# Four sums of the last pair on VectorE, and a matmul of the forget gates one token tile later

## The chip, the cores and the metric

The kernel runs on one core of a Trainium2 chip. The metric is the device time of one execution in microseconds (us), as a median over runs. The engines are named as in the profile: PE is TensorE (PEld its weight loads), DVE is VectorE, ACT is ScalarE, POOL is GpSimd, and SP is SyncE, which only issues transfers here. L1408 means line 1408 of the kernel before.

## The reference

A decoder trunk of two layers on 1024 tokens of width 1024. Layer 0 mixes tokens by sparse attention, layer 1 by attention with forget gates; both end with a gated ConvFFN. Two places of it matter here: the ConvFFN's last product, and the forget gates of layer 1.

```python
def conv_ffn(h, w_up, conv_w, conv_b, w_down):      # D_FF = 2816
    u = h @ w_up                                     # 1024 x 5632
    u = lax.conv_general_dilated(u, conv_w[:, None, :], ...) + conv_b   # causal, depthwise, width 3
    a, b = u[..., :D_FF], u[..., D_FF:]
    return (jax.nn.silu(a) * b) @ w_down             # 1024 x 2816 @ 2816 x 1024

# reference(), before layer 1
hs = rms_norm(x, kv_norm) @ w_kv_shared              # keys, values, 12 gate columns
log_f = jax.nn.log_sigmoid(hs[..., 2 * MIX_W:].astype(jnp.float32) + b_fgate.astype(jnp.float32))
dcum = jnp.cumsum(log_f, axis=1).transpose(0, 2, 1)  # added to the attention's scores
```

## The kernel before

**Precision.** Every f32 operand of a large matmul is split into a high and a low half (`split`: ACT writes the high half at L81, DVE the low half at L82), and a product is three matmuls (`mm3`, L157 to L159).

**The ConvFFN.** Both of its products are computed with seven block products in place of eight, so sums of blocks are needed on each side. `Up` makes the hidden values in 22 chunks of 128 columns, as tiles of 128 columns by 1024 tokens (names `v`). Two neighbouring chunks `g` and `h` make a pair; there are 11 pairs, numbered 0 to 10. `left(k)` makes the left factors of pair k: four of the seven are sums (`s1`, `s2`, `s4` and an upper half of `g`, written in place), made by the four adds of L1408 to L1411 on tiles of 128x512, and three are the halves of `g` and `h` themselves. `store(k)` writes all seven to DRAM (`gd`, L1417), in the order of `self.factors`: two halves of `v` first, then `s2` and the rest. For pairs 0 to 9 the sums lie in tiles `gs`, for pair 10 in tiles `ws`.

**The down product.** `Down` works in steps: one step is one block product i of one pair j, 12 matmuls of 128x512 (four row blocks, three matmuls each). The steps are, in order, product 0 with pairs 0 to 9 (steps 0 to 9 here), product 1 with pairs 0 to 9 (steps 10 to 19), product 0 and product 1 with pair 10 (steps 20 and 21), and then the other five products (step 22 on). A step needs a left factor, read back from `gd` into a tile `wr` (`fetch`, L1508; one tile holds the factors of two steps; there are three such tiles), and a block of `w_down` (in tiles `hx` and `hT`, loaded at L1497). `prep` splits both into a `wh` and a `wl`, of which there are four each: the split of step n + 4 can start when PE has left step n. Sums of `w_down` blocks for later steps are adds on DVE (L1529, L1531, L1533).

**What sets the order.** Within `Up.run` the instructions of DVE and ACT keep the order in which the code records them, by slots (`manual_schedule` in `gated`): pair 10 has `left` in slot 164 and `store` in slot 166, the down steps start in slot 160. On POOL, PE and SP a scheduler sets the order when the kernel is built, as it does for all that is recorded after `Up.run`; of that it fills some in ahead, such as the sums L1529. Each engine works through its own list in that order. SP's is the one queue for all transfers: a transfer that waits for its data holds up all that stand behind it. The factors of pair 10 and the fetches of the following steps stand like this on SP in layer 0 (`gd_10` is the DRAM tile of pair 10, and `wr_11351` takes the factors of steps 14 and 15); the change leaves these rows as they are:

```order
L1508 DMA wr_11304<-gd_2_9070 128x512
L1508 DMA wr_11304<-gd_3_9353 128x512
L1417 DMA gd_10_11337<-v_11048 128x512
L1417 DMA gd_10_11337<-v_11178 128x512
L1417 DMA gd_10_11337<-ws_11292 128x512
L1417 DMA gd_10_11337<-v_11048 128x512
L1417 DMA gd_10_11337<-v_11178 128x512
L1417 DMA gd_10_11337<-ws_11292 128x512
L1417 DMA gd_10_11337<-ws_11293 128x512
L1508 DMA wr_11351<-gd_4_9636 128x512
L1508 DMA wr_11351<-gd_5_9919 128x512
L1508 DMA wr_11406<-gd_6_10202 128x512
```

The fetches for steps 14 to 19 stand behind the store of pair 10.

**The forget gates.** `middle` ends with two rounds over the eight token tiles: the first round (n = 0) computes the first part of the values and the gate columns `z`, the second (n = 1) the rest of the values; a tile is 24 matmuls of 128x390 (`layer1_v`). Around the second round stands the generator `forget`, in three parts. Part one turns `z` into log sigmoids `lsg`, on ACT and with some 17 small instructions on DVE (L992 to L1003). Part two makes their running sum with four matmuls against a triangle and ones (L1008, L1009) and a few small adds (L1013, L1014). Part three transposes the result (L1020) and stores it to `dd` (L1026), which the attention reads later (L1079, L1087). L1198 says ahead of which tile each part comes: 0, 2 and 4.

## Time and profile before

| | |
|---|---|
| median of 3 runs | 2561.35 us (2555.23 to 2565.48) |
| profiled execution, its own time | 2560.4 us |
| its span in the trace | 2558.4 us |
| mean granted clock of PE | 0.993 |
| busy: PE, PEld | 2460.7 us, 2052.7 us |
| busy: DVE, ACT, POOL | 1868.4 us, 1345.1 us, 764.1 us |

The span runs from the first to the last instruction in the trace; the 2.0 us beside it are the start and end of an execution. A row of the timeline reads: start in us, duration in us, engine, line, operation, tile written and tiles read, shape, count, and in brackets how long the engine was idle before and what ended that. A row of the chain of waits has start, duration, and what the chain ran through; "issue" is time in which the engine waited for nothing that the profile shows. Matmuls overlap, so the duration of one (0.39 us) is longer than the distance from its start to the next start.

### The profile page before, as it was taken

The page shows a single profiled execution, that of the slowest core. Times are in us where ns is not written, and L with a number is a line of the kernel's source. Part 1 is how long each engine was busy: PE and PEld are TensorE (multiplying, and loading weights), DVE is VectorE, ACT ScalarE, POOL GpSimd, SP SyncE. Part 2 cuts the span into 40 slices and gives each one's busy share as a digit, 9 for nine tenths or more (in the row PEclk, how much of TensorE's full clock was granted, in tenths as well). Part 3 has the DMA queues.
Part 4 walks back from the last instruction along what each step waited for, and adds up shares of the span by engine and source line. Part 5 has one row for each costly group of instructions (what it writes and reads, how often), then busy time and mean ns, then how long its engine had stood idle before and what let it go on. Part 6 is the DMA issues. An engine that isn't in the chain of part 4 may idle for free.

```text
span 2558.4 us, 35716 instructions
## 1 busy us (share of the span) xinstructions
PE 2460.7 (96%) x12306; PEld 2052.7 (80%) x12306; DVE 1868.4 (73%) x3180; ACT 1345.1 (53%) x2565; POOL 764.1 (30%) x620
## 2 busy tenths in 40 slices
PE   7898999988999999999999999999999999999998
PEld 7787877776878888887888988887777888888787
DVE  5758888887377787777765467878476778878766
ACT  5337777876244454444454356767235444444444
POOL 0104444544034555543000000000234455454000
PEclk9999999999999999999999999999999999999999
DMA  8473234344423333357334466665622233337623
GB/s 251 141 217 113 66 86 116 105 117 131 149 79 102 100 112 99 101 178 280 100 124 149 150 188 189 194 185 169 217 106 86 95 104 111 99 100 263 206 91 123
DMA packets 303276, 357.68 MB, mean 140 GB/s; under 512 B 38024, under 2 KB 183288, under 8 KB 303096
## 3 DMA queue, kind: packets, MB, share of 16 engines
q1 hardware_dynamic: 303096, 355.41, 44.2%
q8 instruction: 97, 1.59, 0.3%
q14 instruction: 83, 0.68, 0.1%
HBM read 245.55 MB, written 109.78 MB: 139 GB/s over the span
## 4 chain that ended last, share of the span: by engine, by line
PE 73%; DVE 8%; ACT 6%; DMA 5%; issue 3%; POOL 3%; SPq 1%; POOLq 0%; ACTq 0%; DVEq 0%
PE psa L157 11%; PE psa L158 11%; PE psa L159 11%; PE psb L157 9%; PE psb L159 9%; PE psb L158 9%; PE psb L399 4%; PE psa L300 4%; PE psb L422 4%; DVE pt L409 2%; POOL ws L1408 2%; ACT pt L406 1%; DMA hT<-in_w_down_dram 1%; DVE ps L330 1%; DVE wl L82 1%
## 5 line engine op out<-in xcount | busy, mean ns | idle before, releaser
L81 ACT ACTIVATE wh<-wr 128x512 fp32r<-128x512 f32 (+2 forms) x254 | 192.7, 763 | 336.4 <-PE psb L159 141.6
L82 DVE TENSOR_TENSOR wl<-wr,wh 128x512 fp32r<-128x512 f32 (+2 forms) x254 | 242.1, 957 | 151.1 <-ACT wh L81 150.4
L1389 DVE SCALAR_TENSOR_TENSOR v<-u,cw,v 128x1023 f32<-128x1023 f32 (+1 forms) x176 | 271.7, 1544 | 69.0 <-ACT v L1387 68.8
L409 DVE TENSOR_TENSOR pt<-psb,pt 128x512 fp32r<-128x512 f32 (+2 forms) x380 | 246.8, 659 | 66.5 <-ACT pt L406 63.4
L1387 ACT ACTIVATE v<-u,cw 128x1024 f32<-128x1024 f32 x88 | 109.6, 1246 | 310.3 <-DVE u L1376 283.6
L406 ACT ACTIVATE pt<-psb 128x512 fp32r<-128x512 f32 (+2 forms) x380 | 213.3, 572 | 87.6 <-PE psb L399 81.3
L422 PE MATMUL psb<-pt,vv 128*128 128x512 f32 (+2 forms) x864 | 225.7, 356 | 18.5 <-DVE pt L409 12.8
L159 PE MATMUL psa<-hT,wl 128*128 128x512 f32 x560 | 218.0, 389 | 0.8 <-DVE wl L82 0.8
L157 PE MATMUL psa<-hT,wh 128*128 128x512 f32 x560 | 218.4, 391 | 0.0
L158 PE MATMUL psa<-hT,wh 128*128 128x512 f32 x560 | 217.9, 389 | 0.0
L300 PE MATMUL psa<-kk,qq 128*128 128x512 f32 (+4 forms) x792 | 184.7, 347 | 13.9 <-DVE stat L330 6.9
L121 POOL TENSOR_TENSOR rs<-ss,consts 128x1 f32<-128x1 f32 x40 | 22.8, 570 | 555.5 <-DVE ss L119 347.5
L422 PEld LDWEIGHTS psb<-pt,vv 128*128 128x128 f32 x864 | 141.0, 191 | 43.9 <-DVE pt L409 21.1
L343 ACT ACTIVATE ps<-ps,stat 128x128 f32<-128x128 f32 (+1 forms) x192 | 147.8, 771 | 46.6 <-DVE stat L330 46.3
L481 POOL TENSOR_TENSOR wr<-wr 128x512 f32<-128x512 f32 x32 | 42.0, 1318 | 428.0 <-ACT pt L406 243.7
L157 PE MATMUL psb<-hT,wh 128*128 128x512 f32 x384 | 156.7, 408 | 1.0 <-DVE pt L409 0.9
L399 PE MATMUL psb<-consts,ps 128*128 128x128 f32 x928 | 148.4, 277 | 8.1 <-DVE pt L409 3.3
L159 PE MATMUL psb<-hT,wl 128*128 128x512 f32 x384 | 151.4, 394 | 0.0
L158 PE MATMUL psb<-hT,wh 128*128 128x512 f32 x384 | 150.7, 393 | 0.0
L330 DVE CUSTOM_DVE_ANT_0 ps<-psa,caub 128x128 f32<-128x128 f32 (+1 forms) x192 | 138.9, 750 | 15.2 <-PE psa L300 14.9
L300 PEld LDWEIGHTS psa<-kk,qq 128*128 128x128 f32 x792 | 120.3, 191 | 30.3 <-DVE stat L330 10.3
L157 PE MATMUL psa<-hx,wh 128*128 128x512 f32 x368 | 144.0, 392 | 0.4 <-ACT u L1379 0.4
(300 smaller groups left out, 6759.3 us busy)
## 6 DMA issues: line engine op xcount, KB each, us to landing
wr<-in_w_up_dram SPq DMA_DIRECT2D x88, 512.0 KB
wr<-gd SPq DMA_DIRECT2D x154, 256.0 KB
gd<-v SPq DMA_DIRECT2D x88, 256.0 KB
o<-ob SPq DMA_DIRECT2D x128, 128.0 KB
wr<-o SPq DMA_DIRECT2D x32, 512.0 KB
hT<-in_w_down_dram SPq DMA_DIRECT2D x64, 256.0 KB
gd<-gs SPq DMA_DIRECT2D x60, 256.0 KB
qd<-st SPq DMA_DIRECT2D x56, 256.0 KB
```

The lines of the kernel that those rows point to most:

```text
L81: nc.scalar.activation(hi, src, AF.Copy)
L82: nc.vector.tensor_tensor(lo, src, f32(hi), ALU.subtract)
L157: mm(out, lh, rh, start=first, stop=False, skip_group_check=more)
L158: mm(out, lh, rl, start=False, stop=False, skip_group_check=more)
L159: mm(out, ll, rh, start=False, stop=last, skip_group_check=more)
L300: nc.tensor.matmul(out, w, rhs, start=b not in banks[:i], stop=b not in banks[i + 1:])
L330: self.nc.vector.tensor_tensor_reduce(p, s, br["spans"][ii][2], -1.0, 3e38, ALU.add, ALU.min, br["stat"][:, 0, ii:ii + 1])
L399: nc.tensor.transpose(tp[0:kb, x:x + P], br["pt"][ii][:, o:o + kb], self.ident)
L406: nc.scalar.activation(st["hi"], st["src"], AF.Copy)
L409: self.nc.vector.tensor_tensor(st["lo"], st["src"], f32(st["hi"]), ALU.subtract)
L422: self.nc.tensor.matmul(out, v, t, start=st["begin"] and i == 0, stop=st["end"] and i == len(mms) - 1)
L1389: nc.vector.scalar_tensor_tensor(v[:, d:], u[:, :S - d], cw[:, tap, i:i + 1], v[:, d:], ALU.mult, ALU.add)
```

## The change

The four adds of pair 10 run on DVE in place of POOL, in both layers, and parts two and three of `forget` come ahead of tiles 3 and 5 in place of tiles 2 and 4.

```diff
@@ middle
                     for t in range(NT):
-                        if t % 2 == 0:
+                        if t in (0, 3, 5):
                             next(forget, None)
                         self.layer1_v(vp, h, 1, t, w1, self.psb()[:, 0:390], fb, z)
@@ left
             s1, s2, s4 = two[0][:, 0], two[0][:, 1], two[1][:, 0]
-        add = self.k.nc.gpsimd.tensor_tensor
+        add = (self.k.nc.gpsimd if k < NF // 2 - 1 else self.k.nc.vector).tensor_tensor
         add(s1, g[:, CH:], h[:, CH:], ALU.add)
```

On DVE, at the end of layer 0's up product, the difference reads as follows. `wl_11275`, `wl_11299` and `wl_11320` are the low halves of steps 6, 7 and 8; `v_11048` and `v_11178` are `g` and `h` of pair 10.

```order
 L82 TENSOR_TENSOR wl_11275<-wr_11102,wh_11274 128x512
 L82 TENSOR_TENSOR wl_11275<-hx_10966,wh_11274 128x512
+L1408 TENSOR_TENSOR ws_11292<-v_11048,v_11178 128x512
+L1529 TENSOR_TENSOR hx_11005<-hT_11122 128x512
+L1409 TENSOR_TENSOR ws_11292<-ws_11292,v_11048 128x512
+L1410 TENSOR_TENSOR v_11048<-v_11048 128x512
+L1411 TENSOR_TENSOR ws_11293<-v_11178,ws_11292 128x512
 L82 TENSOR_TENSOR wl_11299<-wr_11102,wh_11298 128x512
 L82 TENSOR_TENSOR wl_11299<-hx_10966,wh_11298 128x512
-L1529 TENSOR_TENSOR hx_11005<-hT_11122 128x512
 L82 TENSOR_TENSOR wl_11320<-wr_11187,wh_11319 128x512
 L82 TENSOR_TENSOR wl_11320<-hx_11005,wh_11319 128x512
```

The four adds, and one sum of `w_down` blocks with them, now stand ahead of the low halves of step 7; the sums L1529, L1531 and L1533 that follow move back by a few rows against the splits. Layer 1 has the same difference, and the four adds are gone from POOL's list in both layers.

On PE, in the second round over the token tiles, the matmuls of the running sum stand between these two tiles before (`psb_13382` is tile 1, `psb_13433` tile 2):

```order
L158 MATMUL psb_13382<-bl_13188,hT_12455 128x390
L159 MATMUL psb_13382<-bh_13187,hT_12456 128x390
L1008 MATMUL psb_13415<-lsg,tri 128x96
L1009 MATMUL psb_13416<-lsg,tri 128x96
L157 MATMUL psb_13433<-bh_13163,hT_12455 128x390
```

With the change tile 2 is `psb_13415` and tile 3 `psb_13466`:

```order
L158 MATMUL psb_13415<-bl_13188,hT_12455 128x390
L159 MATMUL psb_13415<-bh_13187,hT_12456 128x390
L1008 MATMUL psb_13448<-lsg,tri 128x96
L1009 MATMUL psb_13449<-lsg,tri 128x96
L157 MATMUL psb_13466<-bh_13163,hT_12455 128x390
```

The 24 matmuls of tile 2 have moved ahead of the running sum. The transposes L1020 move past tile 4 in the same way, and on SP the store to `dd` moves behind the three value stores of tile 4; on DVE and ACT the splits of tile 2 now stand among the adds L1013.

## The prediction

> **What bounds the kernel now.** I read the page's chain of waits first, then that chain in order of time, then the engines around its longest piece that is not a matmul.

> The shares of the chain, by engine:

> ```profile
> PE 73%; DVE 8%; ACT 6%; DMA 5%; issue 3%; POOL 3%; SPq 1%; POOLq 0%; ACTq 0%; DVEq 0%
> ```

> PE bounds the kernel. An edit off PE is therefore worth only what it takes away of PE's waits. The chain in time shows where POOL's 3% lie:

> ```profile
> 1165.17 1.15 DVE v L1396
> 1166.45 20.27 POOL ws L1408
> ...
> 1191.24 3.78 DMA wr<-gd
> ...
> 2344.12 20.28 POOL ws L1408
> ```

> One add of pair 10 takes 20.27 us, the same in layer 1 (20.28). Behind it the chain runs through the other adds and the store to a fetch that lands in 3.78 us. The view of line 1408 says what such an add takes otherwise:

> ```profile
> L1408 POOL TENSOR_TENSOR gs<-v,v x20: 1291/1291/1303, 791.4 to 2312.3; 128x512 f32<-128x512 f32 x20
> L1408 POOL TENSOR_TENSOR ws<-v,v x2: 20270/20274/20279, 1166.4 to 2344.1; 128x512 f32<-128x512 f32 x2
> ```

> Same shape, 1.29 us for the 20 other pairs. What differs is DVE beside it. In its timeline it has no gap from L1396 until the two sums that start at 1184.28, and it then stands idle for 10.21 us:

> ```profile
> 1167.42 0.68 DVE L82 TENSOR_TENSOR wl<-wr,wh 128x512 fp32r<-128x512 f32 x1
> ...
> 1184.28 1.28 DVE L1531 TENSOR_TENSOR hx<-hx,hx 128x512 f32<-128x512 f32 x2
> 1195.78 0.69 DVE L82 TENSOR_TENSOR wl<-wr,wh 128x512 fp32r<-128x512 f32 x1 [10.21 <-ACT wh L81]
> ```

> POOL's add ends at 1186.72, 1.16 us after DVE's last sum ends (1185.56): it got through when DVE paused. So I take the other 19 us for waiting on DVE's stream of two-input adds. [...]

> What the 20 us hold up is seen on SP (its waits, then its timeline):

> ```profile
> SPq L1417 <- POOL ws L1409: 15.6, 1, 15.6
> ```
> ```profile
> 1168.50 2.31 SPq L1508 DMA_DIRECT2D wr<-gd  x4
> 1171.14 1.01 SPq L1417 DMA_DIRECT2D gd<-v  x2
> ...
> 1191.24 3.14 SPq L1508 DMA_DIRECT2D wr<-gd  x6
> ```

> After two stores, SP waits for `s2`, and the fetches for steps 14 to 19 stand behind it. In windows of the trace (us; DVE busy; PE clock; DMA share; GB/s) the transfers have nothing to do meanwhile:

> ```profile
> 1172.00:1176.00 4.00, 4.00 (x8) 1.00 0.84 311
> 1176.00:1188.00 12.00, 9.57 (x16) 1.00 0.00 1
> ```

> Last, PE: matmuls before the stall and the first at full pace after it, in both layers, and windows with PE's clock in the column behind the count:

> ```profile
> 1181.79 0.39 PE L157 MATMUL psa<-wh 128*128 128x512 f32 x1
> ...
> 1192.44 0.39 PE L159 MATMUL psa<-wh,wl 128*128 128x512 f32 x1
> 1196.32 0.79 PE L157 MATMUL psa<-wh 128*128 128x512 f32 x1 [3.49 <-ACT wh L81]
> ...
> 1202.33 0.40 PE L158 MATMUL psa<-wl,wh 128*128 128x512 f32 x1
> ...
> 2370.12 0.39 PE L159 MATMUL psa<-wh,wl 128*128 128x512 f32 x1
> ...
> 2379.96 0.39 PE L159 MATMUL psa<-wh,wl 128*128 128x512 f32 x1
> ```
> ```profile
> 1196.32:1202.33 6.01, 5.99 (x14) 0.51 0.93 340
> 2373.55:2379.96 6.41, 6.39 (x15) 0.51 1.03 368
> ```

> At 1181.79 PE turns to the banks of product 1: step 10. By 1192.44 it has started 48 matmuls, steps 10 to 13, so one start costs (1192.44 - 1181.79) / 47 = 0.2266 us and a step 2.72 us. It stalls exactly ahead of step 14, the first whose factor SP held back. After the stall the granted clock is 0.51 for 6 us.

> **The adds moved to DVE: what goes.** In layer 0 the 14th start after 1192.44 falls at 1202.33; at full pace it would fall 14 x 0.2266 = 3.17 us after. Lost: 9.89 - 3.17 = 6.72 us. In layer 1 the 15th start after 2370.12 falls at 2379.96: 9.84 - 3.40 = 6.44 us. In layer 0, 3.65 us of it are the wait (1192.67 to 1196.32) and 3.07 us the slow clock behind it. [...]

> **What the adds cost on DVE.** DVE's list, in the trace of before, from the end of L1396 to the first add into x (L1565):

> ```profile
> 1166.22:1220.55 54.33, 42.59 (x72) 0.94 0.69 243
> ```

> 72 instructions in 42.59 us: 0.59 us each of this shape. Four adds are 2.4 us per layer, and the order puts them and one sum, five instructions or 3.0 us, ahead of step 7's low halves, which stood at 1167.42. They then end at about 1171.7. PE needs them for step 7, three steps before step 10: 1181.79 - 3 x 2.72 = 1173.63. The slack left is 1.9 us, and it grows afterwards, because the order lets the next splits pass the sums. What hid DVE's lateness so far was the 10.21 us of idleness in the stall; that cover goes with the stall. Without it the stretch has 54.33 - 6.72 = 47.6 us for 42.6 + 2.4 = 45.0 us of work. DVE is filled to 94%, and still ahead of PE: nothing is added, with an upper bound in the rivals. A gain beyond the stall is excluded, since PE starts a matmul every 0.2266 us on both sides of it.

> The adds read what DVE itself wrote just before, so L1408 waits for no other engine. The sums are ready at about 1170.5, before SP arrives at them (1172.15); the five other stores take SP some 2.5 us, at the 0.5 us of the first two, so the fetch for steps 14 and 15 goes out at about 1175 in place of 1191.24. It lands 4 to 5 us later (3.78 in the chain above), by 1180. ACT can use it when PE leaves step 10, at 1184.5, and PE needs it at 1192.67. More than 10 us are to spare. The fetch for steps 12 and 13 waits for the tile that step 7's split frees, so it goes out 3.0 us later than before, with PE's need at 1187.2. SP's later transfers, x among them, move forward into the window with DMA share 0.00. POOL loses four instructions and nobody waits for it there any more.

> **The running sum one tile later.** The rows are PE's tile 1, its wait, the instruction on DVE that ends it, and the next ones in line:

> ```profile
> 1418.13 0.34 PE L157 MATMUL psb<-bh,hT 128*128 128x390 f32 x1
> ...
> 1422.24 0.34 PE L159 MATMUL psb<-bh,hT 128*128 128x390 f32 x1
> 1425.19 0.43 PE L1008 MATMUL psb<-lsg,tri 128*128 128x96 f32 x2 [2.60 <-issue]
> 1434.28 1.03 PE L1020 MATMUL psb<-consts,z 128*12 128x128 f32 x8
> ```
> ```profile
> 1424.84 0.25 DVE L1003 SCALAR_TENSOR_TENSOR lsg<-lsg 128x96 f32<-128x96 f32 x1
> 1427.58 0.26 DVE L1014 TENSOR_TENSOR z<-psb,offs 128x96 f32<-128x96 f32 x1
> ```

> Tile 1 has 24 matmuls, 23 distances in 4.11 us: 0.179 each, 4.29 a tile. PE is ready at 1422.42 and waits until 1425.19: 2.77 us. With tile 2 ahead it arrives at 1426.7, when L1003 is 1.6 us past, so the whole 2.77 us go and no more can. The lower end is 0, if tile 2's own bank held PE; but four banks rotate, and tile 2 takes one that the first round's tile 6 left long ago. Next in line, L1014 comes some 2 us later than before (L1009 moves by 1.5, two splits of tile 2 stand among the adds) at about 1429.5; L1020 then stands at about 1435.8. Its wait stays hidden. ACT, DVE and SP see the same work, and `dd` is stored about 1.5 us later.

> **The sum.** 6.72 + 6.44 + 2.77 = 15.9 us of 2560.4 us, the profiled execution's own time: 2544.5. That execution lies 1.0 us under the median of the runs shown (2561.35), so 2545 for the median, 0.6% faster. A measurement of this kernel tells about 0.5% from no change, which is 12.8 us (2548.5).

> **The rivals.**
> - *DVE saturates.* If an instruction costs the 0.68 us that its row lists and not the pace of 0.59, 76 of them take 51.7 us where PE leaves 47.6: 4.1 us per layer come back, 2545 + 8 = 2553. It decides from 0.626 us on. Against it stands the pace in the window above, with the same kinds of instruction.
> - *The transfers are late instead.* The seven stores go out at 1172, when DMA is still at a share of 0.84, and the fetches for steps 12 to 15 queue behind. If one takes 15 us, PE stalls as before, clock included, and only the forget gates' 2.8 us remain: 2558. Against it: the fetch in the chain landed in 3.78 us, as the first of a burst of six.
> - *Held tile (slower).* The 20 us were not DVE's doing but a wait for the tile `ws`, still in use until about 1185.4 (1186.72 less 1.29). Then L1408 stands as long at the head of DVE, in order, with step 7's low halves behind it. These end at 1185.4 + 5 x 0.59 + 1.2 = 1189.6, and PE, due at 1173.63, loses 16 us and 3 us of clock where it lost 6.6: 12.4 us more per layer, 2561 + 24.8 - 2.8 = 2583. It decides once L1408 is held over 2 us. For it: of all pairs only pair 10 uses `ws`. Against it: the row is busy time, not idle time ahead of the add, and it ends with DVE's pause in both layers.

> **Chances.** The forecast 0.76 (2539 to 2551 with the runs' spread of 0.2% to either side); DVE saturates or a part of a stall stays, 0.14; late transfers 0.05; held tile 0.05. The range goes from 2538 to 2555, through most of the second case. Faster by over 0.5%: eight tenths of the forecast and a quarter of the second, 0.65; within: the rest of these and the late transfers, 0.30; slower 0.05.

> **What would show it.** Right: DVE has L1408 to L1411 at 0.6 us each, SP has no wait of 15 us at L1417, PE starts step 14 with no gap and a clock of 1.00 in both layers, and L1008 follows tile 2 without idle time. Wrong: a bracket on L1408 in DVE's timeline, PE waits ahead of any of steps 7 to 22 on `wl` or on `wr<-gd`, or a new wait at L1020.

## The result and the profile after

The changed kernel took 2547.96 us (median of 8 runs, 2545.76 to 2554.23) and the kernel before 2561.95 us (median of 8, 2555.23 to 2565.84) beside it: 14.0 us less, ratio 0.995, 95% interval 0.9936 to 0.9963. The forecast was 2545. The profiled execution of the changed kernel took 2553.19 us, with a span of 2551.4 us and a mean granted clock of 0.992.

The page's chain of waits, by engine: PE's share is up from 73% to 78%, and POOL's is down from 3% to 1%.

```profile
PE 78%; DVE 8%; ACT 6%; DMA 3%; issue 3%; POOL 1%; SPq 0%; POOLq 0%; ACTq 0%; DVEq 0%
```

The view of line 1408 (shortest, median and longest in ns): pair 10's add is now DVE's, at 0.69 us in place of 20.27.

```profile
L1408 POOL TENSOR_TENSOR gs<-v,v x20: 1287/1288/1301, 797.9 to 2311.2; 128x512 f32<-128x512 f32 x20
L1408 DVE TENSOR_TENSOR ws<-v,v x2: 689/689/689, 1174.0 to 2344.0; 128x512 f32<-128x512 f32 x2
```

DVE's timeline at the end of layer 0's up product (this execution reaches the place 6.54 us later than the one of before, from a stretch that lies ahead of the change). No row has a bracket, so nothing waits; a row lasts 0.69 us and the next starts 0.60 us after it. The two rows at 1176.97 and 1177.57 are step 7's low halves.

```profile
1171.62 1.22 DVE L1396 TENSOR_TENSOR v<-v,v 128x1024 f32<-128x1024 f32 x1
...
1173.95 0.69 DVE L1408 TENSOR_TENSOR ws<-v,v 128x512 f32<-128x512 f32 x1
1174.56 0.69 DVE L1529 TENSOR_TENSOR hx<-hT 128x512 f32<-128x512 f32 x1
1175.16 0.69 DVE L1409 TENSOR_TENSOR ws<-ws,v 128x512 f32<-128x512 f32 x1
...
1176.97 0.69 DVE L82 TENSOR_TENSOR wl<-wr,wh 128x512 fp32r<-128x512 f32 x1
1177.57 0.69 DVE L82 TENSOR_TENSOR wl<-hx,wh 128x512 fp32r<-128x512 f32 x1
```

The windows from the end of L1396 to the first L1565, in both layers (busy us of PE, PEld, DVE, ACT and POOL with their counts, then PE's clock, DMA share, GB/s): PE is busy throughout at a clock of 1.00, and DVE for 44.7 of 47.6 us.

```profile
1172.75:1220.31 47.56, 47.56 (x212) 39.37 (x211) 44.74 (x75) 20.23 (x36) 0.00 (x0) 1.00 0.82 281
2342.80:2390.34 47.54, 47.54 (x212) 39.37 (x211) 44.71 (x75) 20.21 (x36) 0.00 (x0) 1.00 0.82 286
```

SP's timeline: the seven stores go out without a pause, and the fetches for steps 14 to 19 right behind them.

```profile
1175.17 3.30 SPq L1508 DMA_DIRECT2D wr<-gd  x4
1178.52 0.90 SPq L1417 DMA_DIRECT2D gd<-v  x2
1179.47 0.50 SPq L1417 DMA_DIRECT2D gd<-ws  x1
1180.01 2.00 SPq L1417 DMA_DIRECT2D gd<-v  x2
1182.06 1.34 SPq L1417 DMA_DIRECT2D gd<-ws  x2
1183.49 7.63 SPq L1508 DMA_DIRECT2D wr<-gd  x6
```

And PE at the forget gates' running sum: L1008 follows tile 2 with no idle time.

```profile
1426.39 0.34 PE L159 MATMUL psb<-bh,hT 128*128 128x390 f32 x1
1426.57 0.35 PE L1008 MATMUL psb<-lsg,tri 128*128 128x96 f32 x2
```

Whole spans vary from one execution to the next, so I compare stretches between fixed instructions. Three of them hold the change: from the start of pair 10's L1396 to the first L1565 in each layer ("layer 0", "layer 1"), and from L1003 to the first load of `dd` ("forget"; it is L1079's, some us ahead of L1087's). All are in us from one profile of each kernel.

| kernel | layer 0 | layer 1 | forget | median | before, beside it | ratio (95%) |
|---|---|---|---|---|---|---|
| before | 55.47 | 55.16 | 40.34 | | | |
| after | 48.69 | 48.69 | 37.50 | 2547.96 | 2561.95 | 0.9950 (0.9936-0.9963) |
| after_again | 48.69 | 48.71 | 37.51 | 2550.13 | 2563.20 | 0.9947 (0.9934-0.9961) |
| adds_only | 48.69 | 48.69 | 42.01 | 2552.22 | 2566.63 | 0.9950 (0.9934-0.9965) |
| forget_only | 55.05 | 54.72 | 37.50 | 2561.74 | 2566.63 | 0.9984 (0.9974-0.9994) |
| stores_by_pool | 61.68 | 62.15 | 41.89 | 2581.91 | 2566.63 | 1.0056 (1.0037-1.0074) |
| dve_waits_for_pool | 50.14 | 50.17 | 40.37 | 2557.12 | 2566.63 | 0.9963 (0.9949-0.9978) |
| two_more_adds | 48.71 | 48.70 | 37.51 | 2551.38 | 2563.20 | 0.9950 (0.9937-0.9963) |
| four_more_adds | 50.33 | 50.29 | 37.51 | 2551.04 | 2563.20 | 0.9954 (0.9940-0.9969) |
| twelve_more_adds | 61.43 | 61.82 | 37.49 | 2574.60 | 2563.20 | 1.0045 (1.0028-1.0062) |
| one_memset | 48.71 | 48.71 | 41.93 | 2558.38 (one) | 2563.55 (one) | |
| one_copy | 54.44 | 54.56 | 41.90 | 2567.88 (one) | 2563.55 (one) | |
| memset_and_forget | 48.71 | 48.70 | 37.51 | 2551.74 | 2565.40 | 0.9942 (0.9929-0.9956) |
| one_column_memset | 48.70 | 48.70 | 37.50 | 2552.18 | 2565.40 | 0.9948 (0.9935-0.9960) |

Wherever PE does not wait, the layers' stretch is 48.69 to 48.71 us. That makes it a sharp measure: what stands above 48.7 is what PE lost. Where PE waits it is less sharp: forget_only has the stalls of the kernel before, and its two stretches are 0.42 and 0.44 us shorter.

### The profile page after: what moved, and what is told of

It is laid out like the page before. It is cut to its first block, busy times and chain, and to the rows that moved or that the text cites. A ratio compares the mean times of both kernels' runs of the same rounds, so it can differ in the third digit from the quotient of the medians.

```text
span 2551.4 us, 35699 instructions
## 1 busy us (share of the span) xinstructions
PE 2460.2 (96%) x12306; PEld 2054.1 (81%) x12306; DVE 1881.4 (74%) x3188; ACT 1347.0 (53%) x2565; POOL 716.1 (28%) x612
## 4 chain that ended last, share of the span: by engine, by line
PE 78%; DVE 8%; ACT 6%; DMA 3%; issue 3%; POOL 1%; SPq 0%; POOLq 0%; ACTq 0%; DVEq 0%
PE psa L157 12%; PE psa L158 12%; PE psa L159 12%; PE psb L157 10%; PE psb L159 10%; PE psb L158 10%; PE psa L300 4%; PE psb L399 4%; PE psb L422 3%; DVE pt L409 2%; ACT pt L406 2%; DVE ps L330 1%; ACT ps L343 1%; PE psb L905 1%; DVE wl L82 1%
## 5 line engine op out<-in xcount | busy, mean ns | idle before, releaser
L81 ACT ACTIVATE wh<-wr 128x512 fp32r<-128x512 f32 (+2 forms) x254 | 192.9, 763 | 325.3 <-PE psb L159 146.9
L82 DVE TENSOR_TENSOR wl<-wr,wh 128x512 fp32r<-128x512 f32 (+2 forms) x254 | 242.4, 958 | 134.4 <-ACT wh L81 133.8
L1389 DVE SCALAR_TENSOR_TENSOR v<-u,cw,v 128x1023 f32<-128x1023 f32 (+1 forms) x176 | 277.9, 1579 | 69.0 <-ACT v L1387 68.7
L159 PE MATMUL psa<-hT,wl 128*128 128x512 f32 x560 | 218.0, 389 | 0.8 <-DVE wl L82 0.8
L157 PE MATMUL psa<-hT,wh 128*128 128x512 f32 x560 | 218.4, 391 | 0.0
L158 PE MATMUL psa<-hT,wh 128*128 128x512 f32 x560 | 217.9, 389 | 0.0
L157 PE MATMUL psb<-hT,wh 128*128 128x512 f32 x384 | 157.4, 410 | 1.4 <-DVE pt L409 1.2
L159 PE MATMUL psb<-hT,wl 128*128 128x512 f32 x384 | 152.1, 396 | 0.0
L158 PE MATMUL psb<-hT,wh 128*128 128x512 f32 x384 | 151.5, 394 | 0.0
L157 PE MATMUL psa<-hx,wh 128*128 128x512 f32 x368 | 144.1, 392 | 0.5 <-ACT u L1379 0.5
```

Source lines behind the costliest of these rows:

```text
L81: nc.scalar.activation(hi, src, AF.Copy)
L82: nc.vector.tensor_tensor(lo, src, f32(hi), ALU.subtract)
L157: mm(out, lh, rh, start=first, stop=False, skip_group_check=more)
L158: mm(out, lh, rl, start=False, stop=False, skip_group_check=more)
L159: mm(out, ll, rh, start=False, stop=last, skip_group_check=more)
L1389: nc.vector.scalar_tensor_tensor(v[:, d:], u[:, :S - d], cw[:, tap, i:i + 1], v[:, d:], ALU.mult, ALU.add)
```

## Experiments: each half by itself

```diff
# adds_only
-        add = self.k.nc.gpsimd.tensor_tensor
+        add = (self.k.nc.gpsimd if k < NF // 2 - 1 else self.k.nc.vector).tensor_tensor
# forget_only
-                        if t % 2 == 0:
+                        if t in (0, 3, 5):
```

> Only the four adds of pair 10 on DVE; the forget gates as before. By the prediction's terms (6.72 us in layer 0, 6.44 us in layer 1) 13.2 us less than before, 0.5%: L1408 of pair 10 takes 0.6 to 0.7 us on DVE, PE has no wait ahead of step 14, and the 2.8 us of idle time ahead of L1008 stay. If the two edits only help together, or if the adds on DVE moved a wait elsewhere that the other edit covers, it is less than 10 us.

> Only the forget gates' parts two and three one token tile later; the adds as before. By the prediction 2.8 us less than before, 0.1%, which lies inside the runs' spread, so the trace decides: L1008 follows tile 2's last matmul without idle time, and the stretch from L1003 to the first load of dd (L1087) is 2.8 us shorter, while both PE stalls of 6.7 and 6.4 us in the two layers stay. The rival, a wait that only moves to L1020 or to the load of dd, leaves that stretch as long as before.

The halves are independent. With the adds alone both layers have the changed kernel's 48.69 us; with the forget gates alone the two stalls are there and the forget stretch is the changed kernel's 37.50. In time the first gave 14.4 us between the medians, the second 4.9 (by its ratio 1.5 to 6.7 us, where 2.8 were expected).

The forget stretch of adds_only held a surprise: with the same wait of 2.6 us as before it is 42.01 us and not 40.34. Windows behind the wait, of adds_only and then of before, with PE's clock in the column behind the counts:

```profile
1423.80:1427.01 3.21, 3.21 (x11) 3.21 (x12) 2.47 (x13) 0.00 (x0) 0.00 (x0) 0.51 0.70 222
```
```profile
1425.19:1428.40 3.21, 3.21 (x20) 3.21 (x21) 2.47 (x13) 0.00 (x0) 0.00 (x0) 1.00 0.76 238
```

In the one, PE ran 3.2 us at 0.51 after it; in the other, at full clock. Of the six profiles that have this wait, four show the long stretch (41.89 to 42.01 us) and two the short one (40.34 and 40.37). The edit is thus worth 2.84 us or some 4.4; the last section shows what the difference goes with.

## Experiments: what held POOL's add, and what carried it to PE

**Another issuer for the stores.** The seven stores of pair 10 leave SP's queue; the adds stay on POOL.

```diff
-            self.k.nc.sync.dma_start(gd[j], t)
+            (self.k.nc.sync if k < NF // 2 - 1 else self.k.nc.gpsimd).dma_start(gd[j], t)
```

> The adds stay on POOL and the forget gates as before; only the seven stores of pair 10 are issued by POOL in place of SP. Theory (DVE's stream holds POOL's add, and SP's order carries that wait to PE): L1408 still takes some 20 us on POOL, but SP has no wait of 15.6 us at L1417, the fetches for steps 14 to 19 go out by about 1176 us, and PE's stall ahead of step 14 is gone in both layers: 11 to 13 us less than before, as long as pair 10's factors, stored at about 1195, are read back before steps 20 and 21 start at 1209. Rival (the fetches could not have gone earlier anyway, for want of a free tile or of bandwidth): the stall ahead of step 14 stays, and the time is that of before, within 3 us.

This was slower, against the theory's number. The rows of POOL, DVE, SP's wait and PE say why:

```profile
1172.87 26.28 POOL L1408 TENSOR_TENSOR ws<-v,v 128x512 f32<-128x512 f32 x1 [13.44 <-DVE v L1396]
```
```profile
1196.71 1.28 DVE L1533 TENSOR_TENSOR hT<-hT,hx 128x512 f32<-128x512 f32 x2
1213.82 0.69 DVE L82 TENSOR_TENSOR wl<-wr,wh 128x512 fp32r<-128x512 f32 x1 [15.82 <-ACT wh L81]
```
```profile
SPq L1149 <- DMA gd<-v: 27.3, 1, 27.3
```
```profile
1204.30 0.39 PE L159 MATMUL psa<-wh,wl 128*128 128x512 f32 x1
1214.36 0.80 PE L157 MATMUL psa<-wh 128*128 128x512 f32 x1 [9.68 <-ACT wh L81]
```

The fetch for steps 14 and 15 was free (SP sent it at once) and PE got through both: from step 10 at 1188.20 it started 72 matmuls, six steps, without a gap. But with PE running, DVE did not pause either, and the add was held longer, 26.28 us, until 1.16 us after DVE's last instruction ended (1197.99). On SP the next row was no longer a store but the first load of `x` (L1149), which waited 27.3 us for the stores of `v`, with the fetches for step 16 on behind it: these stores now stood in POOL's list, and three of the four went out behind the held add, from 1199.10 on. So PE stalled two steps later and for longer. Both parts of the theory hold, the hold by DVE's stream and the queue that carries it; what failed was the count of what stands in that queue.

**A pause for POOL.** DVE gets a copy of one column of `s4`, so that it stands until POOL is done.

```diff
         add(s4, h[:, :CH], s2, ALU.subtract)
+        if k == NF // 2 - 1:
+            self.k.nc.vector.tensor_copy(self.k.sb(self.pool, [P, 1], F32, "dm", 1), s4[:, 0:1])
```

> The adds stay on POOL; DVE gets one more instruction behind its first two sums, a copy of one column of s4 to a tile that nobody reads, so that DVE pauses there until POOL's four adds are done. Theory (POOL's add runs as soon as DVE pauses): L1408 ends some 1.3 us after DVE's pause begins (at about 1168.6), the four adds are done at about 1173.7, step 7's low halves at 1175.0 where PE wants them at 1173.9, so PE waits about 1.2 us there per layer at full clock and the stall ahead of step 14 is gone: some 10 us less than before. Rival (the tile ws was held until 1185.4 by something else): DVE stands until about 1190.6, PE loses 18 us and the slow clock per layer where it lost 6.6, some 25 to 30 us more than before.

The line's view, DVE's pause and PE's only wait at these steps (line numbers below the edit are 2 higher):

```profile
L1408 POOL TENSOR_TENSOR ws<-v,v x2: 3413/3414/3414, 1174.0 to 2346.0; 128x512 f32<-128x512 f32 x2
```
```profile
1175.61 0.69 DVE L1531 TENSOR_TENSOR hx<-hT,hT 128x512 f32<-128x512 f32 x1
1181.35 0.15 DVE L1413 COPY dm<-ws 128x1 f32<-128x1 f32 x1 [5.05 <-POOL ws L1411]
```
```profile
PE psb L158 <- DVE wl L82: 1.2, 1, 1.2
```

DVE's stream ended at 1176.30 and POOL's add at 1177.45, 1.15 us later, as in the kernel before (1.16) and in stores_by_pool (1.16): three times it came through when DVE paused, wherever that was. PE waited the 1.2 us expected, and 9.5 us between the medians are close to the 10 expected. The same add into the same tile `ws` took 3.4 us, so nothing else held the tile.

**One instruction in the stream that reads nothing.** The adds stay on POOL; behind step 6's low halves DVE gets one instruction into an unused half tile.

```diff
         add(s4, h[:, :CH], s2, ALU.subtract)
+        if k == NF // 2 - 1:
+            self.k.nc.vector.memset(two[1][:, 1], 0.0)            # one_memset
+            self.k.nc.vector.tensor_copy(two[1][:, 1], g[:, :CH]) # one_copy, in place of it
```

> The kernel before (adds on POOL), with one memset on DVE behind step 6's low halves, of 128x512 into a half tile that nobody reads: an instruction without any SBUF input in the middle of DVE's stream of two-input instructions. Theory A (POOL needs only an instruction on DVE that leaves its inputs alone): L1408 ends within some 1.3 us of the memset's start and takes 2 to 3 us in place of 20.27, and then L1409 is held in its place until DVE pauses at about 1186, so the time is that of before within 3 us. Theory B (POOL needs DVE idle): L1408 takes 20 to 21 us as before and L1409 1.3.

> The same with a copy of 128x512 from SBUF to SBUF in place of the memset: one SBUF input in place of two. Theory A1 (what holds POOL is the second SBUF input): L1408 gets in as with the memset, 2 to 3 us, and L1409 is held in its place. [...]

POOL and DVE of one_memset, and line 1408 of one_copy (L1413 is the added instruction; line numbers below it are again 2 higher):

```profile
1173.26 2.20 POOL L1408 TENSOR_TENSOR ws<-v,v 128x512 f32<-128x512 f32 x1 [25.18 <-ACT wh L81]
1175.54 1.62 POOL L1409 TENSOR_TENSOR ws<-ws,v 128x512 f32<-128x512 f32 x1
1177.13 1.74 POOL L1410 TENSOR_TENSOR v<-v 128x512 f32<-128x512 f32 x1
1178.83 1.74 POOL L1411 TENSOR_TENSOR ws<-v,ws 128x512 f32<-128x512 f32 x1
```
```profile
1174.38 0.48 DVE L1413 MEMSET ws<- 128x512 f32 x1
1174.78 1.24 DVE L82 TENSOR_TENSOR wl<-wr,wh 128x512 fp32r<-128x512 f32 x1
1175.94 1.78 DVE L82 TENSOR_TENSOR wl<-hx,wh 128x512 fp32r<-128x512 f32 x1
1177.64 1.78 DVE L82 TENSOR_TENSOR wl<-wr,wh 128x512 fp32r<-128x512 f32 x1
1179.34 1.77 DVE L82 TENSOR_TENSOR wl<-hx,wh 128x512 fp32r<-128x512 f32 x1
1181.04 0.68 DVE L1531 TENSOR_TENSOR hx<-hT 128x512 f32<-128x512 f32 x1
```
```profile
L1408 POOL TENSOR_TENSOR ws<-v,v x2: 20605/20605/20605, 1171.2 to 2352.2; 128x512 f32<-128x512 f32 x2
```

The memset let L1408 in, as theory A had it; the copy with one SBUF input did not: L1408 took 20.61 us there, so A1 fails. The second half of A was wrong: L1409 was not held in its place. Once POOL was in, the two engines took turns until its four adds were done, POOL's at 1.6 to 1.7 us in place of 1.29 and DVE's at 1.77 us in place of 0.69, and each pair was through in 1.70 us. PE lost nothing (48.71 us). The 20 and 26 us, through some 30 and 40 instructions of DVE at 0.60 us each, show that POOL's add stayed out from one instruction of DVE's unbroken stream to the next.

> One memset of 128x512 on DVE as in one_memset, the adds on POOL, and the forget gates one tile later. In one_memset the stretch from L1396 of pair 10 to the first L1565 was 48.71 us in both layers, the same as in the changed kernel. So the time is that of the changed kernel, some 14 us less than before. If POOL's adds, which held DVE for 1.1 us each there, cost something elsewhere, it is less.

> The same with a memset of one column (128x1) in place of 512. Theory C (any instruction without SBUF input in DVE's stream lets POOL in, however short): L1408 takes some 2 us and the stage 48.7 us, as with 512 columns, 14 us less than before. Theory D (the hole has to be long enough, the 0.4 us of the full memset): L1408 takes 20 to 21 us, the stall ahead of step 14 is back with 6 us per layer, and only the forget gates' 2.8 us are won.

One column is enough: L1408 took 2.21 us in both, the layers 48.70 and 48.71, and the times are those of the changed kernel (0.9942 and 0.9948; 0.9947 and 0.9950 for the change itself). DVE's rows in one_column_memset, where 0.06 us of an instruction opens the stream:

```profile
1173.02 1.77 DVE L82 TENSOR_TENSOR wl<-wr,wh 128x512 fp32r<-128x512 f32 x1
1173.04 0.06 DVE L1413 MEMSET ws<- 128x1 f32 x1
```

So theory C holds for a memset of 0.06 us, and the gain does not depend on moving the adds. No version beat the changed kernel.

## Experiments: how much room DVE had

Two, four or twelve more adds of the same shape stand behind the four, on DVE, into an unused half tile; all else is the changed kernel, which ran beside them as after_again.

```diff
         add(s4, h[:, :CH], s2, ALU.subtract)
+        if k == NF // 2 - 1:
+            for _ in range(2):      # 4, 12
+                add(two[1][:, 1], g[:, :CH], h[:, :CH], ALU.add)
```

> The changed kernel itself once more, beside the next three on one chip: 12 to 16 us less than before.

> The changed kernel with two more adds of the same shape on DVE behind the four, in both layers, into a half tile that nobody reads. The order puts one sum of w_down blocks between them, so step 7's low halves come three instructions, 1.8 us, later than in the changed kernel, where they end 2.0 us ahead of PE's need. Theory (only what stands ahead of the next low half counts, and 2.0 us of slack are there): PE waits at most 0.2 us at step 7, and the time is that of the changed kernel. Rival (DVE is already full over the stretch): the 1.2 us of added work show in full in PE's time in each layer, 2.4 us in all.

> The same with four more adds; the order puts three sums among them, so step 7's low halves come seven instructions, 4.2 us, later than in the changed kernel. Theory: slack 2.0 us, so PE waits 2.2 us per layer at step 7 at full clock, 4.4 us over the changed kernel, and nothing further on, because the sums that were drawn forward are missing later. Rival (what counts is DVE's total over the stretch, 45.0 + 2.4 us of work in 47.6): no difference from the changed kernel.

> The same with twelve more adds; the order puts eleven sums among them, so step 7's low halves come 23 instructions, 13.7 us, later. Theory: PE waits 11.7 us at step 7 in each layer and runs at about half clock for some 6 us after it, which costs 3 us more: 14.7 us per layer, 29 us over the changed kernel, some 15 us over before. Rival (the total counts: 45.0 + 7.2 us of work in 47.6): 4.6 us per layer, 9 us over the changed kernel, still below before.

Two more cost nothing. PE in four_more_adds at step 7, and PE's waits in twelve_more_adds (total, times, longest; its L1568 is L1565 of the kernel before):

```profile
1173.94 1.07 PE L157 MATMUL psb<-wh 128*128 128x512 f32 x4
1176.31 0.51 PE L158 MATMUL psb<-wl,wh 128*128 128x512 f32 x1 [1.30 <-DVE wl L82]
```
```profile
PE psb L158 <- DVE wl L82: 9.9, 1, 9.9
PE psa L157 <- DVE x L1568: 0.6, 1, 0.6
PE psa L157 <- ACT wh L81: 0.3, 1, 0.3
```

Four cost 1.6 us a layer where 2.2 were expected, twelve 12.7 and 13.1 where 14.7 were. The difference is seen in the first row: the scheduler drew all four L157 of step 7, which need no low half, ahead of the first L158, so 3 x 0.2266 = 0.7 us of the lateness is covered. With twelve it drew two matmuls of another step ahead as well, and the clock came back sooner (below). The rival, that DVE's total decides, fails on twelve: 45.0 + 7.2 us in 47.6 would be 4.6 us a layer. What decides is what stands ahead of the next low half that PE needs. In whole times four_more_adds (0.9954) cannot be told from the changed kernel; there only the stretch shows the loss.

## Why the prediction was right, point by point

- **Layer 0, 6.72 us, and layer 1, 6.44 us.** The stretches fell by 6.78 and 6.47. The adds on DVE took away all of both stalls, as adds_only shows, which has the same 48.69 us. That the sizes agree within 0.06 us is luck in part: against the stalls of forget_only (55.05 and 54.72) the gain is 6.36 and 6.03 us.
- **DVE's pace and fill.** 0.60 us an instruction and 44.7 of 47.6 us, as forecast (0.59, and 45.0 of 47.6). The rival "DVE saturates" needed 0.626; the row's 0.69 is not the pace, because rows overlap.
- **Slack ahead of step 7, 1.9 us.** PE's first matmul with a low half, L158, started 0.23 us after the step, at 1180.38, and the low halves ended at 1178.26: 2.1 us. The extra adds confirm it from both sides: 1.8 us more cost nothing, 4.2 us more cost PE 1.3 us behind 0.7 us of matmuls drawn ahead.
- **The fetch for steps 14 and 15** went out at 1183.49, 11.9 us after L1396's start; the forecast's 1175 was 9.9 us after it. The stores began 6.9 us after L1396's start (6.1 before) and took SP 4.9 us where I had counted 3.5. The 10 us to spare hid it, and PE started step 14 without a gap.
- **The forget gates, 2.77 us.** 40.34 to 37.50 is 2.84. L1008 came at 1426.57 (forecast 1426.7) and the wait at L1020 stays hidden: its transposes start at 1435.59 without idle time (forecast 1435.8). This term was too small all the same: in four of six profiles with the wait half a clock follows it, worth another 1.6 us, which the one profile that I had did not show. Only the 2.77 us of the wait itself were foreseen.
- **The sum.** The three stretches give 6.78 + 6.47 + 2.84 = 16.1 us against 15.9. The medians give 14.0, 13.1 with after_again, and 13.7 and 13.2 with the two memset kernels; 16 us lies within each interval that the table gives, but all four lie below. Where 2 us should have gone I can't show: outside the three stretches the profiles differ by more than that with no pattern by kernel (up to pair 10's L1396 in layer 0 from 1165.1 to 1172.7 us).
- **The rivals.** "Held tile" is refuted by dve_waits_for_pool and one_memset, where POOL writes the same tile in 3.4 and 2.2 us. "Late transfers" did not occur: no wait of PE on a fetch in either layer.

## What to carry to other kernels

An instruction that takes 16 times its usual time on an engine off the critical path is worth following: here POOL's add (20.27 us in place of 1.29) starved beside an unbroken stream of DVE, an in-order queue of transfers waited 15.6 us for it, and PE paid 6.78 and 6.47 us. Moving the work to the engine that caused the wait cost PE nothing here: what counted was what stood ahead of that engine's next due result, with 2.1 us of slack, not its total load. Breaking the stream with one memset of 0.06 us did the same. To judge an edit of a half per cent, compare stretches between fixed instructions. They repeated here within 0.05 us where PE did not wait and within 2 us where it did, while whole executions of one kernel varied by 10.

## What the runs showed of the hardware that I had not expected

POOL's f32 add got in neither between DVE's two-input instructions (20.27 us in the kernel before) nor at a one-input copy of f32 (20.61), but at a memset of 0.06 us (2.21), and from then on the two engines took turns. Why the turns do not begin by themselves is open; DVE's rows overlap by 0.09 us in the stream, which would leave no moment free, but no run tested that.

The kernel before has such turns too, at pair 9 of both layers. In layer 0 POOL's L1410 took 2.28 us beside a low half of 128x1024 on DVE and ended 1.16 us after it. What followed on DVE was L1376, an add that reads one input from `psa`, a tile in PSUM, and L1411 (1.74 us) then took turns with the next low halves (1.78 us for the second). It looks as if L1376 gave an opening there that pair 10's stream lacks, but no run tested that either.

PE's clock after a wait does not follow from the wait's length alone. After 1.2 and 1.3 us it stayed at 1.00; after 2.6 us it stayed at 1.00 twice and fell to about half four times; after 3.04 and 3.49 us it was at 0.51 for some 6 us, after 9.86 us at 0.50 for only 4:

```profile
1189.51:1193.52 4.01, 4.01 (x10) 3.15 (x10) 4.01 (x7) 0.19 (x1) 0.00 (x0) 0.50 0.92 296
```

```profile
1420.45:1423.86 3.41, 0.80 (x6) 0.51 (x4) 3.41 (x17) 1.73 (x7) 0.00 (x0) 1.00 0.39 83
1423.86:1427.27 3.41, 3.41 (x12) 3.41 (x13) 2.41 (x13) 0.00 (x0) 0.00 (x0) 0.50 0.69 216
1427.27:1430.68 3.41, 3.41 (x20) 3.41 (x20) 0.00 (x0) 0.27 (x1) 0.00 (x0) 1.00 0.46 136
```
```profile
1420.67:1424.08 3.41, 1.92 (x11) 1.59 (x9) 3.41 (x16) 2.91 (x11) 0.00 (x0) 1.00 0.38 124
1424.08:1427.49 3.41, 2.30 (x14) 2.33 (x15) 3.27 (x18) 0.00 (x0) 0.00 (x0) 1.00 0.91 264
```

In adds_only the whole wait lies in one step, in which PE is busy for 0.80 us, and the next step runs at half. In before the wait is spread over two steps, in which PE is busy for 1.92 and 2.30 us, and the clock stays. The other four profiles fit: 2.61, 2.61 and 2.40 us of idle time in one step (one_memset, stores_by_pool, one_copy) brought half clock, 1.23 and 1.38 us in two steps (dve_waits_for_pool) did not. Over the three stretches of all profiles, half clock followed every step with 2.0 us or more of idle time and none with 1.66 us or less, and full clock came back behind the first step with no more than 0.16 us of it. This also gives the short 4 us above: half clock began at 1183.51, 6.0 us before PE went on, and ended at 1193.75. Elsewhere in the traces the clock also fell after steps with only 1.0 to 1.6 us of idle time, so idle time is not the whole measure, and no run moved a wait along the raster on purpose.
